# Reordering the first head pair's value products in a two-layer attention block

## The chip, the cores and the metric

The kernel runs on one core of a Trainium2 chip. The metric is the device time of one execution in microseconds, from the runs of the whole kernel; the kernel before takes 861.62 us as the median of three runs (859.24 to 862.12).

A core has a matrix engine (TensorE, PE in the profile), a vector engine (VectorE, DVE), an engine for activation functions and copies (ScalarE, ACT), a general-purpose engine (GpSimd, POOL) and SyncE (SP), which here only issues DMAs. Each engine works through its own queue in order; engines meet through semaphores. TensorE writes to PSUM, of which the kernel uses eight tiles (banks) of 128 x 512 float32 numbers; its other tiles lie in SBUF.

## The reference

Two layers work on 512 tokens of 1024 features, in float32:

```python
for i in range(DEPTH):                       # DEPTH = 2
    hn = rms_norm(x, norm_gain[i])
    y = mixer_a(hn, ...) if i % 2 == 0 else mixer_b(hn, ...)
    x = x + y

def mixer_a(...):                            # 3 groups, 16 heads of 64
    proj = hn @ w_in                         # q, k, v of every group, and the gate
    for g, (window, dilation) in enumerate(((128, 1), (512, 4), (2048, 16))):
        q, k = rms_norm(q) , rms_norm(k)     # for each head
        logits = q @ k.T * scale + bias      # inside the dilated window
        out, lse = softmax(logits) @ v, log of the denominator
    y = sum over g of softmax_g(lse) * out   # merged by denominators
    return (y * silu(gate)) @ w_out
```

`mixer_b` has the same outline with one group and a two-dimensional neighbourhood on an 8 x 64 grid of tokens. The softmax over the three groups of layer A, weighted by their denominators, is the same as one softmax over all keys of the three groups, and the kernel computes it so.

## The kernel before, in words

*Products.* A float32 product is made of three `float32r` ones: each operand is split into a high part (`wh`, `hn_h`) and a rest (`wl`, `hn_l`), and `mm3` adds high x high, high x rest and rest x high in PSUM. I call these three matmuls a triple. The normalised input lies in SBUF in both parts. Weights come in blocks of 1024 columns (`wraw`, eight slots) over SP's queue, some of them added up on the way by GpSimd's DMAs. They are used in 360 *jobs* of 512 (or 384) columns: ScalarE copies the high part, and VectorE or GpSimd subtracts to make the rest. Who does it is chosen at line 165 by the pair in `pool[0]`, set at line 296 by the job's number. A rest is made four jobs ahead of its product.

*Pairs.* Heads go in eight pairs (`hc` 0 to 7). In layer A the first pair is projected plainly (`project_qk`). The others use a scheme of seven block products over the two halves of tokens and of features, with sums of the input (`mix_h`, `mix_l`) and sums of weight blocks; `product` is one of these, eight triples in four jobs, and `put11`, `put12`, `put21`, `put22` and others add it up. `main_a(hc)` runs, in this order: `product`, the gate of the pair before (`gate_a`), `product`, v of the pair before (`v0_a`), four products with mixed inputs, the last `product` with `put21`. For `hc` 1, v of the pair before stands ahead of that last product instead.

*Two streams.* `main` projects; `side` does the attention. `run` steps through `main` and lets `side` in between. TensorE executes in the order in which the program emits. The order is set by a clock in nanoseconds that only counts matmuls (`matmul`, `transpose`; 640 for a triple of 512 columns): `yield n` in `side` means "not before n later", `yield "wait", key, n` means "not before n after the stamp of that key", and `later_on(n, job)` emits a job when the clock has passed n. After the first projection the other engines keep the program's order too. A guard (a key that `main` yields) makes `run` emit everything of `side` up to that stamp at once, whatever its due time.

*The attention of one pair in layer A.* `q_a` transposes q and k on TensorE into a bank of PSUM, four times four 128 x 128 blocks, and copies or subtracts each bank to SBUF (`k0h`, `k0l`, `q0h`, `q0l`, `q12`). `k_a` does the same for k of groups 1 and 2 (`k12`). `attn_a` makes the scores in two halves of four banks (`log`); VectorE adds the bias and takes the minimum (the sign is turned), ScalarE takes the exponential and normalises (`p`), and VectorE turns p in 32 x 32 blocks into `pt`. Four `move`s of four DMAs each bring a part of `pt` into a second tile (`t0`); the last stamps `"pt"`. `v_a` transposes v of group 0. `weigh` makes the products of p with v in three thirds, with a `yield 2200` after each of the first two: two thirds read `pt` in place, with v of groups 1 and 2 (`rawk` in the trace); the last reads the moved tile with the transposed v. It holds four banks (`o`). `weighed` multiplies the result by the gate, and the product goes to DRAM (`y_d`).

`log`, `tp` and `o` banks come in turn from one pool of four (`ps_side`).

*Norms of queries and keys.* `head_norm` computes the inverse root on VectorE, and `scale` multiplies the four token blocks by it, each with a `later_on` of its own (line 438).

*What sets the order around the change.* The last quarter of `main_a(2)`'s first product has the guard `("w", 0)`, since its result overwrites v of the first pair; the stamp comes after `weigh` of the first pair. The fifth product of `main_a(2)` has the guard `("q", 1)`, and v of the second pair has `("scored", 1)`, the second half of that pair's scores. For the first pair alone, `attn_a` has `q_a(1)` ahead of `weigh`:

```python
        if hc == 0:
            yield from q_a(hc + 1)
            yield 2500
        yield "wait", ("pt", hc), 11500 if hc == 1 else 9000 if hc == NHC - 2 else 7500
```

For the other pairs it stands behind. At the end of layer A the stored outputs come back (`y_back`) and are split into high part and rest (`y_split`) for the output projection `out_product`, which waits for each of them.

Of the kernel before, what the change touches and what calls it, by code (L numbers as in the profile page):

```python
# [26 lines left out]
NHC = 8  # L27
# [19 lines left out]
def tile_hybrid_encoder(  # L47
# [24 lines left out]
    held = [False]  # L72
# [41 lines left out]
    def bank(name):  # L114

        return ps_side.tile([P, 512], F32, tag="side", name=name)
# [21 lines left out]
    def rsqrt(eng, r, ss, n, scale):  # L138
        v = wk.tile([P, 32], F32, tag="nv", name="nv", bufs=1)
        a = wk.tile([P, 32], F32, tag="na", name="na")  # L140
        eng.tensor_scalar(v[:, :n], ss, scale, EPS, op0=ALU.mult, op1=ALU.add)
        eng.tensor_scalar(
            r.bitcast(I32), v[:, :n].bitcast(I32), -0.5, float(0x5F3759DF), op0=ALU.mult, op1=ALU.add
        )
        for _ in range(3):
            eng.tensor_mul(a[:, :n], r, r)
            if eng is vec:
                eng.scalar_tensor_tensor(a[:, :n], a[:, :n], -0.5, v[:, :n], op0=ALU.mult, op1=ALU.mult)
                eng.scalar_tensor_tensor(r, a[:, :n], 1.5, r, op0=ALU.add, op1=ALU.mult)
                continue  # L150
            eng.tensor_mul(a[:, :n], a[:, :n], v[:, :n])
            eng.tensor_scalar(a[:, :n], a[:, :n], -0.5, 1.5, op0=ALU.mult, op1=ALU.add)
            eng.tensor_mul(r, r, a[:, :n])

    turn, pool = [0], [[2, 5]]

    def cast(raw, n):
        h = wp.tile([P, 512], F32R, tag="wh", name="wh", bufs=6)[:, :n]
        act.copy(h, raw)
        return h, raw, n  # L160

    def rest(h, raw, n):
        l = wp.tile([P, 512], F32R, tag="wl", name="wl", bufs=5)[:, :n]
        turn[0] += 1
        a, b = pool[0]
        eng = pol if turn[0] * a % b < a else vec
        eng.tensor_sub(l, raw, h.bitcast(F32))
        return h, l
# [11 lines left out]
    class Plan:  # L180
# [28 lines left out]
        def add(self, at, dst, off):  # L209

            dst.used(at)
            src = lambda: w[:, off : off + dst.cols]
            self.sums.setdefault(at, []).append(
                lambda: pol.dma_start(dst.tile, src(), accum_op=ALU.add)
            )
# [39 lines left out]
    mixed_jobs = len(plan.jobs)  # L255
# [23 lines left out]
    def load(raw):  # L279
        home(raw)  # L280
        if raw.off is None:
            return
        dst, src = raw.tile[:, : raw.cols], w[:, raw.off : raw.off + raw.cols]
        if not begun:
            syn.dma_start(dst[:, :512], src[:, :512])
            begun.append(load_x(1, 2))
            dst, src = dst[:, 512:], src[:, 512:]
        syn.dma_start(dst, src)
        if behind:
            behind.pop()()  # L290

    def splits():
        casts, queue, due = [], [], plan.loads(lead)
        for at, (raw, c, step, n) in enumerate(plan.jobs):
            first = at - start_jobs
            pool[0] = [0, 1] if first < 16 else [2, 3] if first < 40 else [1, 2] if at < mixed_jobs else [2, 5]
            for r in due.get(at, ()):
                load(r)
            for add in plan.sums.get(at, ()):
                add()  # L300
            casts.append((cast(raw.tile[:, c : c + step], step), n))
            if len(casts) > 1:
                done, m = casts.pop(0)
                queue.append((*rest(*done), m))
            if len(queue) > 4:
                yield queue.pop(0)
        done, m = casts.pop(0)
        queue.append((*rest(*done), m))
        yield from queue

    def steps():
        for h, l, n in splits():
            for c in range(0, h.shape[1], n):
                yield h[:, c : c + n], l[:, c : c + n]
# [11 lines left out]
    def transpose(o, i):  # L326
        clock[0] += 109
        nc.tensor.transpose(o, i, ident)  # L328
# [15 lines left out]
    def later_on(delay, job):  # L344

        timers.append((clock[0] + delay, job))
        timers.sort(key=lambda t: t[0])
# [75 lines left out]
    def head_norm(raw, ss, ns, late):  # L423


        rs = wk.tile([P, 32], F32, tag="rs", name="rs")
        rsqrt(vec, rs[:, : 4 * ns], ss[:, : 4 * ns], 4 * ns, 1.0 / DH)

        def scale(i):
            by = rs[:, i * ns : (i + 1) * ns].unsqueeze(2).to_broadcast([P, ns, 64])  # L430
            v = raw[:, i, : ns * 64].rearrange("p (a b) -> p a b", b=64)
            return vec.tensor_mul(v, v, by)

        if late:
            later.append(lambda: [tc.keep_in_program_order(scale(i)) for i in range(4)])
            return
        for i in range(4):
            later_on(600 + 600 * i, partial(scale, i)) if held[0] else scale(i)

    def transpose4(raw, c):  # L440
        tp = bank("tp")
        for i in range(4):
            transpose(tp[:, i * P : (i + 1) * P], raw[:, i, c : c + P])
        return tp
# [303 lines left out]
            yield from gate_a(hc)  # L748

    def k_a(hc):  # L750
        yield "wait", ("rawk", hc), 9000 if 1 < hc < NHC - 1 else 12000 if hc < 2 else 8000
        k12 = wk.tile([P, 2, 512], F32, tag="k12", name="k12", bufs=1)
        raw = st.pop(("rawk", hc))
        for g in range(2):
            tp = transpose4(raw, g * P)
            act.activation(k12[:, g, :], tp, AF.Copy, scale=gk[:, g + 1 : g + 2])
            yield
        st["k12", hc] = k12, raw[:, :, 256:]

    def q_a(hc):  # L760

        yield "wait", ("rawq", hc), (22000, 10500)[hc] if hc < 2 else 8000
        raw = st.pop(("rawq", hc))
        q0h = wk.tile([P, 512], F32R, tag="q0h", name="q0h", bufs=1)
        q0l = wk.tile([P, 512], F32R, tag="q0l", name="q0l", bufs=1)
        k0h = wk.tile([P, EXT], F32R, tag="k0h", name="k0h", bufs=1)
        k0l = wk.tile([P, EXT], F32R, tag="k0l", name="k0l", bufs=1)
        q12 = wk.tile([P, 2, 512], F32, tag="q12", name="q12", bufs=1)
        tp = bank("tp")
        for i in range(4):  # L770
            transpose(tp[:, i * P : i * P + P].rearrange("p (r j) -> p j r", j=4), raw[:, i, 3 * P :])
        act.activation(k0h[:, 64:EXT], tp, AF.Copy, scale=gk[:, 0:1])
        yield 1000
        vec.scalar_tensor_tensor(
            k0l[:, 64:EXT], tp, gk[:, 0:1], k0h[:, 64:EXT].bitcast(F32), op0=ALU.mult, op1=ALU.subtract
        )
        yield 400
        tp = transpose4(raw, 0)
        act.copy(q0h, tp)
        yield 1000  # L780
        vec.tensor_sub(q0l, tp, q0h.bitcast(F32))
        yield 400
        for g in range(2):
            act.copy(q12[:, g, :], transpose4(raw, P + P * g))
            yield
        stamp["q", hc] = 0
        st["q", hc] = q0h, q0l, q12, k0h, k0l
# [150 lines left out]
    def attn_a(hc):  # L938
# [7 lines left out]
        at = lambda t, hd: 32 * (4 * hd + t)  # L946
# [115 lines left out]
        if last:  # L1062
# [18 lines left out]
            gt = weighed(hc, (yield from weigh()))  # L1081
# [19 lines left out]
        for u in range(2):  # L1101
            for n, tile_ in enumerate(scores(u)):
                later_on(400 + 900 * n, partial(least, n, tile_))
            if u:
                stamp["scored", hc] = 0
                for n in range(4):
                    later_on(8000 + 2000 * n, partial(move, n))
            yield 8500
        fill = bias_rows() if hc == 2 else None
        yield from v_a(hc)  # L1110
        yield "wait", ("pt", hc), 2500
        st["e", hc + 1] = bias_a(hc + 1)
        if hc == 0:
            yield from q_a(hc + 1)
            yield 2500
        yield "wait", ("pt", hc), 11500 if hc == 1 else 9000 if hc == NHC - 2 else 7500
        yield "wait", ("gate", hc), 4000
        gt = weighed(hc, (yield from weigh()))
        if hc < NHC - 2:
            send = lambda: tc.keep_in_program_order(syn.dma_start(y_d[:, hc, :], gt))  # L1120
            later_on(3000, send)
            stamp["w", hc] = 0
            yield
            if fill:
                later_on(1500, fill)
            if hc:
                yield 1500
                yield from q_a(hc + 1)
            return
        st["tail"], back = y_back(range(2), "tr")  # L1130
        stamp["back",] = 0
# [3 lines left out]
        yield from q_a(hc + 1)  # L1135
        _, more = y_back(range(2, NHC - 2), "rawq")
        for n in range(2, NHC - 2):
            later_on(1000 + 2500 * n, partial(y_split, more[:, n - 2, :], n))
        later_on(16000, partial(y_split, gt, hc))

    pending = []

# [378 lines left out]
```

## Time and profile before

| what | value |
|---|---|
| median of the runs | 861.62 us (859.24 to 862.12) |
| the profiled execution's own time | 864.23 us |
| its span, first to last instruction | 862.5 us |
| mean granted TensorE clock | 0.993 |
| TensorE busy | 833.5 us, 97% |
| VectorE busy | 634.5 us, 74% |
| ScalarE busy | 508.2 us, 59% |
| GpSimd busy | 295.6 us, 34% |
| DMA queue q1 (hardware_dynamic) | 108.78 MB, 40.5% of 16 engines |

How to read the rows shown below. A row of a timeline has the start and the duration in us, the engine, the line, the operation, and output<-inputs by the program's names; in brackets stand the idle time ahead of it and what ended it. Nearly all rows have line 85, 324 or 328, those of the helpers that record them, so the names tell the place. A row of windows has the stretch, its length, the busy time of PE, PEld (weight loads), DVE, ACT and POOL with the number of instructions, the granted TensorE clock, the share of the DMA engines, and GB/s. Ends of matmuls are modelled and overlap the next start, so starts are compared.

### The profile page before, as it was taken

How to read it: one execution, taken by the hardware profiler on the slowest of the kernel's cores; microseconds unless marked ns; L12 is line 12 of the kernel's file. 1: busy time of each engine (PE TensorE's matmuls, PEld its weight loads, DVE VectorE, ACT ScalarE, POOL GpSimd, SP SyncE). 2: the span in 40 equal slices, each digit the busy share in tenths (PEclk: the TensorE clock that was granted, in tenths of full speed). 3: DMA queues.
4: the chain of work that ended last, by engine and by line, in shares of the span. 5: the costliest groups of instructions: out<-in, count | busy, mean ns of one | idle time of the engine just before them, and what ended most of it. 6: DMA issues, size and time to landing. Idle time of an engine off the chain costs nothing.

```text
span 862.5 us, 18120 instructions
## 1 busy us (share of the span) xinstructions
PE 833.5 (97%) x6611; PEld 689.0 (80%) x6611; DVE 634.5 (74%) x1650; ACT 508.2 (59%) x1066; POOL 295.6 (34%) x262
## 2 busy tenths in 40 slices
PE   8998988999999999999999999899999999999998
PEld 6875867878877877878877877689998898889776
DVE  7898994787897787787786866547577667866742
ACT  7565672665764955946846828545366644665440
POOL 5043641363362452443543512212223223322301
PEclk9999998999999999999999999999999999999999
DMA  9425754667766775775776664184264456545212
GB/s 337 135 59 139 203 130 121 126 165 198 146 163 199 149 171 168 159 176 175 163 157 190 137 193 144 56 278 144 86 177 144 119 169 182 160 132 137 83 50 98
DMA packets 56169, 131.97 MB, mean 153 GB/s; under 512 B 7184, under 2 KB 24528, under 8 KB 55952
## 3 DMA queue, kind: packets, MB, share of 16 engines
q1 hardware_dynamic: 49744, 108.78, 40.5%
q0 software_dynamic: 6048, 22.02, 15.2%
q8 instruction: 52, 0.85, 0.4%
q14 instruction: 37, 0.30, 0.1%
q10 hardware_dynamic: 288, 0.01, 0.0%
HBM read 111.73 MB, written 11.72 MB: 143 GB/s over the span
## 4 chain that ended last, share of the span: by engine, by line
PE 69%; DVE 10%; ACT 9%; DMA 5%; issue 5%; POOL 1%; ACTq 0%; DVEq 0%; POOLq 0%; SPq 0%
PE acc L324 57%; ACT p L85 5%; PE o L324 5%; PE log L324 4%; DMA wraw<-in_w 4%; PE tp L328 2%; DVE na L85 2%; DVE wl L85 2%; ACT wh L85 2%; ACT rawk L85 1%; DMA yr<-y_d 1%; DVE p L85 1%; DVE rawq L85 1%; DVE rawk L85 1%; DVE gt L85 1%
## 5 line engine op out<-in xcount | busy, mean ns | idle before, releaser
L85 POOL TENSOR_TENSOR wl<-wraw,wh 128x512 fp32r<-128x512 f32 (+1 forms) x157 | 202.3, 1297 | 432.7 <-PE acc L324 216.7
L85 ACT CAST wh<-wraw 128x512 fp32r<-128x512 f32 (+1 forms) x360 | 209.8, 593 | 195.5 <-PE acc L324 150.3
L85 DVE TENSOR_TENSOR wl<-wraw,wh 128x512 fp32r<-128x512 f32 (+1 forms) x203 | 160.1, 792 | 48.4 <-PE acc L324 32.6
L324 PE MATMUL acc<-wh,hn_h 128*128 128x384 f32 (+1 forms) x488 | 185.9, 381 | 3.6 <-DVE gt L85 1.7
L324 PE MATMUL acc<-wl,hn_h 128*128 128x384 f32 (+1 forms) x488 | 177.5, 364 | 2.3 <-DVE wl L85 2.3
L324 PE MATMUL acc<-wh,hn_l 128*128 128x384 f32 (+1 forms) x488 | 177.3, 363 | 0.0
L85 ACT ACTIVATE p<-p,mn 128x256 f32<-128x256 f32 (+2 forms) x248 | 137.9, 584 | 33.5 <-DVE mn L85 33.5
L324 PEld LDWEIGHTS acc<-wh,hn_h 128*128 128x128 f32 x488 | 92.0, 189 | 21.9 <-issue 6.6
L324 PEld LDWEIGHTS acc<-wl,hn_h 128*128 128x128 f32 x488 | 92.2, 189 | 10.8 <-DVE wl L85 3.4
L324 PEld LDWEIGHTS acc<-wh,hn_l 128*128 128x128 f32 x488 | 92.0, 189 | 9.7
L324 PE MATMUL acc<-wl,mix_h 128*128 128x512 f32 x224 | 87.6, 391 | 2.9 <-DVE wl L85 2.2
L324 PE MATMUL acc<-wh,mix_h 128*128 128x512 f32 x224 | 89.0, 397 | 0.0
L324 PE MATMUL acc<-wh,mix_l 128*128 128x512 f32 x224 | 87.4, 390 | 0.0
L324 PE MATMUL acc<-hn_h,wh 128*128 128x512 f32 x192 | 78.6, 410 | 0.3 <-ACT rawb L85 0.2
L324 PE MATMUL acc<-hn_h,wl 128*128 128x512 f32 x192 | 75.1, 391 | 0.0
L324 PE MATMUL acc<-hn_l,wh 128*128 128x512 f32 x192 | 74.9, 390 | 0.0
L85 DVE STREAM_TRANSPOSE pt<-p 128x512 f32<-128x512 f32 (+1 forms) x60 | 40.4, 686 | 22.9 <-ACT p L85 22.8
L85 DVE TENSOR_REDUCE ss<-sq 128x4 f32<-128x256 f32 (+1 forms) x96 | 46.3, 502 | 12.5 <-POOL sq L85 6.2
L324 PEld LDWEIGHTS acc<-wl,mix_h 128*128 128x128 f32 x224 | 42.1, 188 | 12.8 <-DVE wl L85 3.5
L324 PE MATMUL acc<-y_l,wh 128*128 128x512 f32 x128 | 50.1, 392 | 1.9 <-POOL y_l L85 1.9
L324 PE MATMUL acc<-y_h,wh 128*128 128x512 f32 x128 | 51.8, 405 | 0.0
L324 PE MATMUL acc<-y_h,wl 128*128 128x512 f32 x128 | 50.0, 391 | 0.0
(149 smaller groups left out, 1367.2 us busy)
## 6 DMA issues: line engine op xcount, KB each, us to landing
wraw<-in_w SPq DMA_DIRECT2D x95, 512.0 KB
wraw<-in_w POOLq DMA_DIRECT2D x42, 512.0 KB, 7.0
wraw<-in_w SPq DMA_DIRECT2D x38, 384.0 KB
pt<-pt SPq DMA_DIRECT2D x112, 64.0 KB
td<-tr SPq DMA_DIRECT2D x24, 224.0 KB
pt<-td SPq DMA_DIRECT2D x24, 224.0 KB
e<-l_d SPq DMA_DIRECT2D x32, 112.0 KB
e<-l_d SPq DMA_DIRECT2D x16, 128.0 KB
```

The lines of the kernel that those rows point to most:

```text
L85: m = f(*args, **kw)
L324: nc.tensor.matmul(o, l, r, **kw)
L328: nc.tensor.transpose(o, i, ident)
```

## The change

Four groups of numbers and one step's place are changed.

1. Jobs 16 to 39 after the first sixteen of the kernel: GpSimd makes every second rest instead of two of three.
2. `scale(i)` comes due 600 + 1000 i after the norm instead of 600 + 600 i, where it is timed at all (layer A).
3. First pair: `weigh` comes ahead of `q_a(1)`, which now follows it as for the other pairs, after `yield` and `yield 1500`. The moves come due 1300 apart instead of 2000, and `weigh` 4500 after the stamp `"pt"` instead of 7500.
4. Last pair: `k_a` comes due 9000 after its stamp instead of 8000. The splits of the outputs of pairs 2 to 5 come due 2000 sooner, and so does that of pair 6.

```diff
-            pool[0] = [0, 1] if first < 16 else [2, 3] if first < 40 else [1, 2] if at < mixed_jobs else [2, 5]
+            pool[0] = [0, 1] if first < 16 else [1, 2] if at < mixed_jobs else [2, 5]
...
-            later_on(600 + 600 * i, partial(scale, i)) if held[0] else scale(i)
+            later_on(600 + 1000 * i, partial(scale, i)) if held[0] else scale(i)
...
-        yield "wait", ("rawk", hc), 9000 if 1 < hc < NHC - 1 else 12000 if hc < 2 else 8000
+        yield "wait", ("rawk", hc), 9000 if hc > 1 else 12000
...
-                    later_on(8000 + 2000 * n, partial(move, n))
+                    later_on(8000 + (2000 if hc else 1300) * n, partial(move, n))
...
         st["e", hc + 1] = bias_a(hc + 1)
-        if hc == 0:
-            yield from q_a(hc + 1)
-            yield 2500
-        yield "wait", ("pt", hc), 11500 if hc == 1 else 9000 if hc == NHC - 2 else 7500
+        yield "wait", ("pt", hc), (4500, 11500)[hc] if hc < 2 else 9000 if hc == NHC - 2 else 7500
         yield "wait", ("gate", hc), 4000
...
-            if hc:
-                yield 1500
-                yield from q_a(hc + 1)
+            yield 1500
+            yield from q_a(hc + 1)
             return
...
-            later_on(1000 + 2500 * n, partial(y_split, more[:, n - 2, :], n))
-        later_on(16000, partial(y_split, gt, hc))
+            later_on(2500 * n - 1000, partial(y_split, more[:, n - 2, :], n))
+        later_on(14000, partial(y_split, gt, hc))
```

## The prediction

> **What bounds the kernel now.** I read the page first, then the windows, TensorE's waits, and the timelines of the engines where TensorE loses time.
>
> ```profile
> span 862.5 us, 18120 instructions
> PE 833.5 (97%) x6611; PEld 689.0 (80%) x6611; DVE 634.5 (74%) x1650; ACT 508.2 (59%) x1066; POOL 295.6 (34%) x262
> 188.30:251.40 63.10, 62.91 (x653) 50.60 (x652) 53.07 (x130) 40.11 (x79) 28.48 (x24) 1.00 0.70 168
> 125.00:130.00 5.00, 2.43 (x22) 1.62 (x19) 4.76 (x9) 2.17 (x5) 3.25 (x3) 1.00 0.92 186
> 130.00:135.00 5.00, 2.92 (x90) 2.52 (x98) 3.05 (x7) 0.00 (x0) 0.00 (x0) 0.57 0.45 103
> 135.00:140.00 5.00, 5.00 (x113) 4.42 (x102) 0.88 (x4) 0.09 (x1) 0.00 (x0) 0.75 0.43 141
> 112.00:133.00 21.00, 14.80 (x87) 11.30 (x93) 19.82 (x42) 10.92 (x21) 9.88 (x9) 0.95 0.55 117
> 133.00:150.00 17.00, 17.00 (x233) 14.69 (x226) 4.91 (x11) 5.56 (x10) 2.65 (x2) 0.87 0.45 137
> ```
>
> TensorE (PE) is the bound: 862.5 - 833.5 = 29 us idle in all. One whole head pair in the steady part (188 to 251 us) idles 0.2 us, so nothing in an order of work can earn much there. The idle time lies at the first pair: from 125 to 135 us PE works 5.35 of 10 us, and the granted clock falls to 0.57, then 0.75.
>
> ```profile
> 112.78 0.39 PE L324 MATMUL acc<-wh,hn_h 128*128 128x512 f32 x1
> 118.69 0.39 PE L324 MATMUL acc<-wh,hn_h 128*128 128x512 f32 x1
> 120.62 0.50 PE L324 MATMUL acc<-wl,hn_h 128*128 128x512 f32 x1 [1.55 <-DVE wl L85]
> 125.08 1.47 PE L328 MATMUL tp<-ident,rawq 128*128 128x128 f32 x12
> 126.85 0.93 PE L324 MATMUL o<-pt,rawk 32*64 32x128 f32 x8 [0.29 <-ACT q L85]
> 131.84 0.69 PE L324 MATMUL o<-pt,rawk 32*64 32x128 f32 x4 [4.07 <-DVE k0l L85]
> 132.77 3.67 PE L324 MATMUL o<-pt,rawk 32*64 32x128 f32 x116 [0.24 <-DVE q0l L85]
> 136.37 2.60 PE L324 MATMUL o<-pt,v 128*64 128x64 f32 x64
> 138.90 0.50 PE L324 MATMUL acc<-wh,hn_h 128*128 128x512 f32 x1
> 191.42 1.21 PE L324 MATMUL o<-pt,rawk 32*64 32x128 f32 x64
> 198.22 1.97 PE L324 MATMUL o<-pt,v 128*64 128x64 f32 x60
> ```
>
> The first pair's products with v need the four side banks of PSUM, which the second pair's transposes have just filled; the waits named k0l, q0l and q are those banks being emptied. By the code's clock all of it falls due too late: the guard ("w", 0) ahead of the last quarter of the next product flushes twelve transposes and all the products with v in one lump, with no projection between them.
>
> ```profile
> 115.80 1.18 DVE L85 TENSOR_TENSOR na<-rs 128x32 f32<-128x32 f32 x1
> 117.47 2.50 DVE L85 TENSOR_TENSOR rawq<-rawq,rs 128x512 f32<-128x512 f32 x4
> 119.88 1.28 DVE L85 TENSOR_TENSOR wl<-wraw,wh 128x512 fp32r<-128x512 f32 x2
> 123.93 4.37 DVE L85 SCALAR_TENSOR_TENSOR na<-na,nv 128x16 f32<-128x16 f32 x1
> 131.04 0.74 DVE L85 SCALAR_TENSOR_TENSOR k0l<-tp,gk,k0h 128x512 fp32r<-128x512 f32 x1
> 115.59 1.34 POOL L85 TENSOR_TENSOR wl<-wraw,wh 128x512 fp32r<-128x512 f32 x1 [1.90 <-DVE na L85]
> 124.22 4.03 POOL L85 TENSOR_TENSOR wl<-wraw,wh 128x512 fp32r<-128x512 f32 x3
> ```
>
> Why k0l is late: one 16-column step of the norm takes 4.37 us on DVE, just while POOL runs three subtractions (124.22 to 128.25). GPSIMD Engine Reference, Key points, in the Trainium skill says that POOL shares its SBUF interfaces with VectorE and contends with instructions that have two SBUF inputs; this row agrees: 4.37 us for 16 columns, where a rest of 512 columns takes 0.64.
>
> **The change, part by part.** I count code clock (ns) from the end of the first pair's second scores, at 99.71 us. A triple of matmuls adds 640 and takes 0.68 us: 118.69 - 112.78 = 5.91 us for eight triples and four transposes. v's projection ends at 12160, its transposes stand at 14720.
>
> *Products with v ahead of q_a(1).* The four moves are due at 8000, 9300, 10600 and 11900, so "pt" is stamped at 12160 instead of 14080. Adding 4500 gives 16660, and the products start at 17076, one triple before line 740's product ends. Their second third follows 2200 later, at 20063; the last third is flushed by the guard at 22410. So triples lie between the parts, and no transposes of q_a hold the banks. The three waits go: 4.07 + 0.29 + 0.24 = 4.6 us. The products lasted 138.90 - 131.84 = 7.06 us from the wait's end; a later pair's take 1.21 + 1.21 + 1.97 = 4.4, of which I count 4.3 as elapsed, since groups overlap what follows. That is 2.8 us less, since PE no longer runs at the low clock. Together -7.4 us. q_a(1) now falls due after ("w", 0) + 2700, at 26463, between the gate's triples. Its sixteen transposes cost the same; two more interruptions of triples cost about 0.1 us each, and two more for the thirds of the products: +0.4.
>
> *What is late next* is the last third, which reads the moved tile.
>
> ```profile
> 111.17 1.30 DVE L85 STREAM_TRANSPOSE pt<-p 128x512 f32<-128x512 f32 x2
> 112.49 12.23 SPq L85 DMA_DIRECT2D pt<-pt  x16
> 124.77 6.90 SPq L85 DMA_DIRECT2D e<-l_d  x6
> 112.50:113.50 1.00, 1.00 (x6) 0.81 (x6) 0.81 (x2) 1.00 (x3) 1.00 (x1) 1.00 0.09 16
> 113.50:114.50 1.00, 1.00 (x6) 0.84 (x5) 0.90 (x4) 1.00 (x2) 0.19 (x1) 1.00 0.28 66
> 1.18 4.28 DMA hg<-in_head_gain
> ```
>
> The sixteen moves start when the last stream transpose ends (112.47) and leave SP's queue one after another, 0.76 us each, until 124.72. The closer pacing therefore brings no move forward; it brings the stamp forward. No weight load stands between them now, so none is overtaken; the six bias loads follow as before, and the one weight load behind those, issued at job 34, is first used at job 45. The store to y_d moves forward with the products, ahead of the same loads as now. The last third could start at 112.78 + 14 x 0.68 + 0.36 + 2 x 1.14 = 124.9 us. The first move's bytes show about 1.5 us after its issue (16 GB/s, then 66), so the last lands near 126.2: a new wait of 1.3 us. Ends: 0, if it lands as its issue ends, and 124.72 + 4.28 - 124.9 = 4.1, with the slow constant load as the row. I take 1.3, from the row of the same transfer. DMA: Bandwidth & Descriptors, Anatomy of one DMA, in the Trainium skill gives about 2.0 us fixed cost for a DMA; by that the wait would be 1.8, and the sum 0.5 us smaller.
>
> *Scalings 1000 apart instead of 600.* Only VectorE's order changes. The weight rest that PE awaits at 118.69 stands behind four scalings (2.50 us); it will stand behind two, 1.25 us earlier, and a third of the products (1.14) covers PE meanwhile. The 1.55 us wait goes; ends -0.1 and -1.55, since the next item can put VectorE 1.4 us (two rests) late. In later pairs the last scaling comes 1.2 us later, but its readers wait 8 to 12 us after the stamp: 0, from -1.2 (0.2 us of idle in each of six pairs) to as much lost.
>
> *POOL's share in jobs 16 to 39* falls from 16 rests to 12. Four at about 0.65 us move to VectorE, +2.6 us there at most; four POOL runs of 1.3 us fewer can lock it, 5.2 at most. Rests are made four jobs (5.4 us) ahead, which hides it: 0, from -1 to +2.6.
>
> *The second pair's scores.* k_a(1) follows q_a(1) and moves behind three more triples, while the second scores stay at the guard behind v. Seven triples (4.8 us) instead of ten lie between the two.
>
> ```profile
> 151.86 1.18 PE L324 MATMUL log<-k,q 64*32 64x128 f32 x64
> 160.02 0.38 PE L324 MATMUL log<-k0h,q0h 64*128 64x256 f32 x2
> 157.97 0.48 DVE L85 CUSTOM_DVE_ANT_1 p<-log,e,mn 128x256 f32<-128x256 f32 x1
> ```
>
> VectorE releases the last bank at 158.45, 5.5 us after the first scores end (about 152.97). That leaves a wait of 0.7; ends 0 and 2.2.
>
> *Tail.* Splits of the stored outputs start 2000 clock sooner.
>
> ```profile
> 523.96 0.66 PE L328 MATMUL tp<-ident,rawk 128*128 128x128 f32 x4 [1.66 <-DVE k0l L85]
> 541.50 0.50 PE L324 MATMUL acc<-y_l,wh 128*128 128x512 f32 x1 [0.82 <-POOL y_l L85]
> 549.10 0.50 PE L324 MATMUL acc<-y_l,wh 128*128 128x512 f32 x1 [1.11 <-POOL y_l L85]
> ```
>
> Both y_l waits are shorter than the two microseconds given: -1.9. Ends 0, if ScalarE's exponentials keep them in their place, and -3, if the softmax behind them gains too. k_a's 9000 instead of 8000 for the last pair costs nothing: q_a, ahead of it, ends 10.7 us of clock after that stamp, so the 1.66 stays.
>
> Sum: -7.4 + 0.4 + 1.3 - 1.55 + 0.7 - 1.9 = -8.45 us. The profiled execution took 864.23 us, 2.6 above the median of 861.62. From the median: 853.2 us.
>
> **The rivals.**
>
> *Moves too late.* The last third waits 4.1 us instead of 1.3, about the idle time that lowers the clock now, and the 2.8 us of slow products come back: -8.45 + 2.8 + 2.8 = -2.85, 858.8 us. For it: the DMA engines are 0.92 busy from 125 to 130 us. Against: the moves' own lag of 1.5. TensorE: Matmul & The Clock Gate, Part 1, in the Trainium skill says that the clock halves after an idle window of about 3.4 us; the trace agrees as far as it goes (4.07 lowered it to 0.57, 1.55 did not).
>
> *The gain is given back.* The idle stretch lets VectorE catch up: it is busy 19.82 of 21 us up to 133 and only 4.91 of the 17 after. If rests and norms now run late under a busy PE, PE waits for them one by one; at 8 us of such waits the time is about 861. Against: 24.7 us of VectorE work fit in 38 - 8.5 = 29.5, and the rests that PE needs first stand ahead of the norm.
>
> *VectorE becomes the bound (slower).* A rest moved to VectorE can meet a POOL run and be held:
>
> ```profile
> 85.71 2.88 DVE L85 TENSOR_TENSOR wl<-wraw,wh 128x512 fp32r<-128x512 f32 x1 [1.18 <-ACT wh L85]
> L85 DVE TENSOR_TENSOR wl<-wraw,wh 128x512 fp32r<-128x512 f32 (+1 forms) x203 | 160.1, 792 | 48.4 <-PE acc L324 32.6
> ```
>
> If all four take 2.88 us and nothing hides them, they cost 11.5: -8.45 + 11.5 = +3.05, 864.7 us. It decides from 8.5 us of waits on rests. Against: 203 rests on VectorE take 0.79 us in the mean, so held ones are few, and POOL runs less. The contention rule named above speaks for this rival, for the moved rests have two SBUF inputs.
>
> **How the numbers follow.** 0.3% (2.6 us) is about what a measurement of this kernel can tell from no change. The forecast has 0.62 (849 to 857), moves too late 0.15, a still larger gain in the tail and rests (to 847) 0.05; these are faster, 0.82. Given back: 0.10, same. VectorE bound: 0.08, slower. The range takes in the late moves and part of the given-back case: 848.5 to 860.
>
> **What would show it.** Right: products with v in three groups with triples between, ahead of the second pair's rawq transposes; no wait on k0l near 130 us; granted clock 1.00 throughout 120 to 140; a short wait in the group that reads v; no y_l waits near 540. Wrong: that group waits over 3 us at a lower clock; or new waits on wl from 85 to 145 us; or the second scores wait over 2 us for VectorE.

## The result, and the profile after

The changed kernel takes 857.57 us (median of 8 runs, 854.28 to 860.78), the kernel before takes 862.42 in the runs beside it. The ratio is 0.9942, with a 95% interval of 0.9919 to 0.9965: 4.9 us faster (3.0 to 7.0 by the interval), where 8.45 were forecast. The time lies in the forecast range and the sign is right, but the gain is little more than half of the sum. The profiled execution took 857.42 us, against 864.23 before.

The page of the changed kernel, its first lines:

```profile
span 855.6 us, 18127 instructions
PE 833.8 (97%) x6611; PEld 689.7 (81%) x6611; DVE 636.0 (74%) x1654; ACT 508.8 (59%) x1066; POOL 294.5 (34%) x258
```

TensorE (PE) is as busy as before (833.8 against 833.5 us); the span is shorter because PE idles 21.8 us instead of 29.0. The waits of PE from 100 to 187 us (us in total, number, longest), first in the changed kernel, then in the kernel before (one of 0.2 us that both have is left out):

```profile
PE o L324 <- DMA e<-l_d: 2.9, 1, 2.9
PE o L324 <- DMA pt<-pt: 0.5, 1, 0.5
PE tp L328 <- ACT vt L85: 0.2, 1, 0.2
```

```profile
PE o L324 <- DVE k0l L85: 4.1, 1, 4.1
PE acc L324 <- DVE wl L85: 1.5, 1, 1.5
PE acc L324 <- POOL wl L85: 0.8, 1, 0.8
PE o L324 <- ACT q L85: 0.3, 1, 0.3
PE o L324 <- DVE q0l L85: 0.2, 1, 0.2
```

The waits for banks (k0l, q, q0l) are gone, and so is the wait for a weight rest. One wait is new: the products with v wait for a DMA. The timeline of PE in the changed kernel shows which products (start, length, and in brackets the idle time ahead and who ended it):

```profile
117.56 1.21 PE L324 MATMUL o<-pt,rawk 32*64 32x128 f32 x64
121.71 1.21 PE L324 MATMUL o<-pt,rawk 32*64 32x128 f32 x64
124.79 0.39 PE L324 MATMUL acc<-wh,hn_l 128*128 128x512 f32 x1
128.08 0.58 PE L324 MATMUL o<-pt,v 128*64 128x64 f32 x8 [2.90 <-DMA e<-l_d]
129.15 3.25 PE L324 MATMUL o<-pt,v 128*64 128x64 f32 x56 [0.49 <-DMA pt<-pt]
132.33 0.62 PE L324 MATMUL acc<-wh,hn_h 128*128 128x512 f32 x1
155.41 0.38 PE L324 MATMUL log<-k0h,q0h 64*128 64x256 f32 x2
185.75 1.21 PE L324 MATMUL o<-pt,rawk 32*64 32x128 f32 x64
```

The first two thirds run between triples, without a wait. The last third, which reads the moved tile, is ready when the last triple ends (124.79 + 0.39 = 125.18) and gets going at 128.08 and 129.15. The profile puts the first of these waits down to the bias loads, which go through the same queue right behind the moves. The queue of SyncE (SP), and the vector operation (VectorE, DVE) that the first move waits for:

```profile
113.01 11.47 SPq L85 DMA_DIRECT2D pt<-pt  x16
124.53 6.13 SPq L85 DMA_DIRECT2D e<-l_d  x6
112.28 0.70 DVE L85 STREAM_TRANSPOSE pt<-p 128x512 f32<-128x512 f32 x1
```

The sixteen moves are issued from 113.01 to 124.48, and the products go on at 129.15, 4.7 us after the last issue. Windows of the changed kernel (busy time of each engine, then PEclk, the granted clock of TensorE), and of the two long stretches from the first pair's last projection to the second pair's products with v, in the kernel after and then before:

```profile
125.00:130.00 5.00, 1.61 (x25) 1.31 (x26) 4.59 (x15) 1.34 (x3) 2.13 (x2) 0.92 0.88 198
130.00:135.00 5.00, 5.00 (x57) 4.46 (x54) 2.76 (x9) 1.45 (x3) 0.00 (x0) 0.74 0.48 101
515.00:520.00 5.00, 3.11 (x14) 2.20 (x13) 3.79 (x8) 4.93 (x11) 1.31 (x1) 0.83 0.92 348
520.00:525.00 5.00, 5.00 (x88) 4.00 (x87) 2.15 (x7) 3.81 (x5) 2.38 (x2) 0.83 0.18 67
545.00:550.00 5.00, 3.50 (x109) 2.72 (x116) 3.02 (x9) 1.30 (x3) 0.00 (x0) 0.90 0.39 118
550.00:555.00 5.00, 4.96 (x111) 4.12 (x97) 0.92 (x5) 0.49 (x2) 0.00 (x0) 0.75 0.11 18
111.77:185.75 73.98, 70.15 (x617) 56.27 (x615) 58.47 (x141) 46.28 (x90) 32.10 (x26) 0.98 0.63 147
```

```profile
112.78:191.42 78.64, 71.49 (x618) 57.47 (x616) 57.70 (x137) 45.80 (x88) 32.93 (x27) 0.96 0.55 133
```

The stretch became 4.66 us shorter (78.64 to 73.98). PE's idle time in it fell from 7.15 to 3.83 us (-3.3) and its busy time by 1.3, since less of it runs at a low clock. From 186 us to the last pair's step `k_a` at 517 the two kernels need the same time within 1.1 us (331.5 and 332.5). From there the earlier splits of the stored outputs should have shortened the tail:

```profile
517.22 0.66 PE L328 MATMUL tp<-ident,rawk 128*128 128x128 f32 x4 [1.89 <-DVE k0l L85]
546.28 0.66 PE L328 MATMUL tp<-ident,yr 128*128 128x128 f32 x4 [0.89 <-DVE pt L85]
547.95 3.44 PE L324 MATMUL o<-pt,rawk 32*64 32x128 f32 x126 [0.17 <-DVE pt L85]
551.32 2.58 PE L324 MATMUL o<-pt,v 128*64 128x64 f32 x64
```

In the kernel before, the last two groups of these products stood so:

```profile
558.18 0.47 PE L324 MATMUL o<-pt,rawk 32*64 32x128 f32 x13 [1.26 <-issue]
558.58 2.08 PE L324 MATMUL o<-pt,v 128*64 128x64 f32 x64
```

Both waits for y_l (1.9 us) are gone. But from 517.22 to the end of the last products (553.90) it takes 36.7 us, and before it took 36.7 us too (523.96 to 560.66). A wait for pt grew by 0.7 us. And twice the granted clock fell, from 515 to 525 and from 545 to 555 us, where it was 1.00 before: the way from `k_a`'s step to the first transposes of p became 1.2 us longer apart from the y_l wait, and the products that read v 0.5 us longer. The products with rawk lasted about as long as before (3.4 us after 3.7), since the lower clock replaced a gap of 1.26 us for which the profile names no releaser ("issue").

### The profile page after: what moved, and what is told of

It reads as the page before. It is cut to its first block, busy times and chain, and to the rows that moved or that the text cites. A ratio compares the mean times of both kernels' runs of the same rounds, so it can differ in the third digit from the quotient of the medians.

```text
span 855.6 us, 18127 instructions
## 1 busy us (share of the span) xinstructions
PE 833.8 (97%) x6611; PEld 689.7 (81%) x6611; DVE 636.0 (74%) x1654; ACT 508.8 (59%) x1066; POOL 294.5 (34%) x258
## 4 chain that ended last, share of the span: by engine, by line
PE 74%; DVE 9%; ACT 8%; DMA 4%; issue 3%; SPq 1%; POOL 1%; DVEq 0%; ACTq 0%
PE acc L324 61%; ACT p L85 5%; PE o L324 4%; PE log L324 4%; PE tp L328 3%; DMA wraw<-in_w 2%; DVE wl L85 2%; SPq L85 1%; ACT rawk L85 1%; ACT wh L85 1%; DVE na L85 1%; DVE rawq L85 1%; DVE p L85 1%; DVE gt L85 1%; DMA pt<-in_xt 1%
## 5 line engine op out<-in xcount | busy, mean ns | idle before, releaser
L85 POOL TENSOR_TENSOR wl<-wraw,wh 128x512 fp32r<-128x512 f32 (+1 forms) x153 | 197.6, 1292 | 426.8 <-PE acc L324 227.8
```

What stands on the lines that cost most here:

```text
L85: m = f(*args, **kw)
```

## The experiments

*Theories.* The first: the moved tile is late, and the wait for it with the lowered clock behind it takes most of what is missing. Rivals: the gain is given back elsewhere, by work that now waits under a busy PE; and other parts of the change take back what the reorder brings. Ratios are to the kernel before, with a 95% interval.

**Each part alone.** The reorder alone, on the kernel before (the pace of the moves and the last hunk of `attn_a` belong to it):

```diff
-                    later_on(8000 + 2000 * n, partial(move, n))
+                    later_on(8000 + (2000 if hc else 1300) * n, partial(move, n))
...
-        if hc == 0:
-            yield from q_a(hc + 1)
-            yield 2500
-        yield "wait", ("pt", hc), 11500 if hc == 1 else 9000 if hc == NHC - 2 else 7500
+        yield "wait", ("pt", hc), (4500, 11500)[hc] if hc < 2 else 9000 if hc == NHC - 2 else 7500
```

> The kernel before with the third group of the change alone: the first pair's products with v ahead of the second pair's transposes, moves 1300 apart, 4500 after the stamp. If the gain comes from this step, the time falls by 3 to 5 us against before (the changed kernel: 5 us), the k0l wait of 4.07 us is gone, and the last third waits about 3.4 us for its moves at a lower clock. If the gain comes from the other parts, the time stays within 1 us of before.

The scalings alone, the output splits with the later `k_a` alone, and GpSimd's share alone:

```diff
-            later_on(600 + 600 * i, partial(scale, i)) if held[0] else scale(i)
+            later_on(600 + 1000 * i, partial(scale, i)) if held[0] else scale(i)
```

> The kernel before with the second group alone: scalings 1000 apart. By the prediction the wait of 1.55 us on wl at 118.7 us shrinks to about 0.3 and nothing else moves: 1 to 1.5 us faster. If the spread also frees weight rests in every pair, the steady part's waits go too and the time falls by 2 to 3 us. If the transposes' lump at 125 us absorbs what is gained ahead of it, the time stays within 0.8 us.

```diff
-        yield "wait", ("rawk", hc), 9000 if 1 < hc < NHC - 1 else 12000 if hc < 2 else 8000
+        yield "wait", ("rawk", hc), 9000 if hc > 1 else 12000
...
-            later_on(1000 + 2500 * n, partial(y_split, more[:, n - 2, :], n))
-        later_on(16000, partial(y_split, gt, hc))
+            later_on(2500 * n - 1000, partial(y_split, more[:, n - 2, :], n))
+        later_on(14000, partial(y_split, gt, hc))
```

> The kernel before with the fourth group alone: the last pair's k_a at 9000, output splits 2000 sooner. By the prediction the two y_l waits (0.82 and 1.11 us) go and the time falls by 1.9 us. By the rival, that the wait is given back at the products with v that end layer A (a slower clock or later turns there), the y_l waits go and the time stays within 0.8 us of before.

```diff
-            pool[0] = [0, 1] if first < 16 else [2, 3] if first < 40 else [1, 2] if at < mixed_jobs else [2, 5]
+            pool[0] = [0, 1] if first < 16 else [1, 2] if at < mixed_jobs else [2, 5]
```

> The kernel before with the first group alone: four of GpSimd's rests in jobs 16 to 39 go to VectorE. By the prediction 0 (within 1 us). If fewer GpSimd runs free VectorE from being held, the stretch from 85 to 112 us shortens by about 1 us, as in the changed kernel, and the long VectorE rows (2.88 and 1.70 us) get fewer. If VectorE is the bound there, it is 1 to 2.6 us slower.

| kernel | median us | ratio |
|---|---|---|
| reorder alone | 857.04 | 0.9938 [0.9917, 0.9959] |
| scalings alone | 861.47 | 0.9985 [0.9973, 0.9996] |
| output splits and `k_a` alone | 862.61 | 1.0000 [0.9985, 1.0016] |
| GpSimd's share alone | 862.78 | 1.0005 [0.9988, 1.0022] |
| whole change | 857.57 | 0.9942 [0.9919, 0.9965] |

The reorder alone is as fast as the whole change. GpSimd's share does nothing. The scalings bring 1.3 us (0.3 to 2.3 by the interval), and without the reorder not by the route that I forecast. In the waits from 60 to 140 us of the kernel with the scalings alone the wait for the rest at 118.7 us has shrunk from 1.55 to 0.3 us (the 2.1 us in the list lies ahead of 85 us), but the bank wait named q has grown from 0.3 to 1.6 us:

```profile
PE o L324 <- DVE k0l L85: 4.2, 1, 4.2
PE acc L324 <- DVE wl L85: 2.5, 2, 2.1
PE o L324 <- ACT q L85: 1.6, 1, 1.6
```

What this trace does gain ahead of the second pair lies elsewhere: from the transposes of rawq at 67.5 us to the first pair's second scores it takes 0.6 us less (67.53 to 97.19, before 67.50 to 97.74), where two waits for k of 0.3 and 0.7 us are gone.

The splits alone do in their trace what they are for, and their time still doesn't move. Their timeline, from `k_a`'s step to the last products:

```profile
522.99 0.66 PE L328 MATMUL tp<-ident,rawk 128*128 128x128 f32 x4 [1.39 <-DVE k0l L85]
550.98 0.66 PE L328 MATMUL tp<-ident,yr 128*128 128x128 f32 x4 [0.89 <-DVE pt L85]
555.69 0.47 PE L324 MATMUL o<-pt,rawk 32*64 32x128 f32 x14 [0.95 <-issue]
556.09 2.08 PE L324 MATMUL o<-pt,v 128*64 128x64 f32 x64
```

No wait for y_l is left, one for pt has grown from 0.17 to 0.89 us, and at full clock the stretch takes 35.2 us (522.99 to 558.17) instead of 36.7. Of the 1.5 us that this execution shows, 0.3 is a shorter gap without a releaser between the last products (0.95 instead of 1.26 us); the rest, 1.93 - 0.72 = 1.2 us, is less than the interval of the ratio can tell from nothing (1.3 us on either side).

**The price of the late tile.** The last third of the first pair reads the turned tile in place of the moved one, so nothing in this pair waits for the moves:

```diff
-                        lambda hd, d=run * a + 256 * ia + 32 * ta, m=m: sb(t0, d + 128 * hd, [[m, 2], [1, 32]]),
+                        lambda hd, d=run * a + 256 * ia + 32 * ta, m=m: sb(t0 if hc else pq, d + 128 * hd, [[m, 2], [1, 32]]),
```

> The changed kernel, with the last third of the first pair's products reading the turned tile in place (pq) instead of the moved tile (t0). The moves are still issued, nobody in the first pair waits for them; left out is that these products read the exchanged data. Theory, the wait and the clock cost the rest of the gain: the 2.90 + 0.49 us of waiting in front of the last third go, and so does the low granted clock of 125 to 135 us (o<-pt,v took 4.25 us from start to the next matmul, against 2.0 at full clock), together 5.4 us: about 852 us, ratio to the kernel before near 0.988, granted clock 1.00 from 120 to 135 us, and the second pair's second scores begin near 150 us instead of 155.4. Rival, given back: the work behind the wait (the second pair's scores, which need VectorE) waits in the wait's place, the time stays within 856 to 858 us.

It took 850.66 us, ratio 0.9850 [0.9824, 0.9876]. Its timeline:

```profile
118.12 1.21 PE L324 MATMUL o<-pt,rawk 32*64 32x128 f32 x64
125.69 2.08 PE L324 MATMUL o<-pt,v 128*64 128x64 f32 x64
150.79 0.38 PE L324 MATMUL log<-k0h,q0h 64*128 64x256 f32 x2
181.16 1.21 PE L324 MATMUL o<-pt,rawk 32*64 32x128 f32 x64
```

From the first third to the second pair's products it takes 63.0 us (118.12 to 181.16), in the changed kernel 68.2 (117.56 to 185.75): the late tile costs 5.2 us, of which 3.4 are the wait. The second pair's second scores come 4.6 us earlier and wait for nothing, so this time isn't given back. The clock stayed at 1.00 from 115 to 140 us. The medians differ by more, 6.9 us; in this pair of profiles 1.1 us of the rest lies in the tail, where the clock did not fall behind `k_a`'s step. The first theory stands, and its rival falls.

**What makes it late.** First without the two loads that GpSimd's queue adds up on the way while the moves travel:

```diff
     def add(self, at, dst, off, left_out=False):
             dst.used(at)
+            if left_out:
+                return
...
-                self.add(j + 3 + 2 * i, b11[i], b12[i].off)
+                self.add(j + 3 + 2 * i, b11[i], b12[i].off, hc == 2)
```

> The changed kernel without the two accumulating loads that GpSimd's queue issues at 120.2 and 123.5 us, while the moves travel (left out: the bias slab's two sums of this stage are not added in). Theory, the accumulating loads hold the moves up: the last moved piece lands near 127 instead of 129.15 us, the wait of the last third falls from 3.4 to 1.3 us and the clock is kept, about 853 us. Rival, the issue on SP's queue sets the landing (16 issues, 113.01 to 124.48, 0.72 us each, and some us behind the last): the wait stays at 3.0 to 3.4 us, about 857.5 us.

It took 850.86 us, ratio 0.9863 [0.9838, 0.9888]. Its timeline of SP and of PE:

```profile
113.71 10.64 SPq L85 DMA_DIRECT2D pt<-pt  x16
126.88 2.09 PE L326 MATMUL o<-pt,v 128*64 128x64 f32 x64
```

The moves are issued by 124.35, and at 126.88 the last third needs no wait: the tile is there 2.5 us after the last issue or sooner, against 4.7 in the changed kernel. In the five other profiles of this order that show the landing it came 3.0 to 5.8 us after the last issue, so the accumulating loads are probably a part of the lateness; it is one profile, and whether their 512 KB each or the adding does it isn't separated. (The two sums left out are of weight blocks of the third pair, not of a bias.) A reservation: in this run a rest came 0.86 us late, which put the reader itself back by as much and can hide a wait of that size.

Then with the second pair's bias loads later in the written order:

```diff
-        st["e", hc + 1] = bias_a(hc + 1)
+        if hc:
+            st["e", hc + 1] = bias_a(hc + 1)
...
             stamp["w", hc] = 0
+            if hc == 0:
+                st["e", hc + 1] = bias_a(hc + 1)
```

> The changed kernel with the second pair's six bias loads (e<-l_d, 124.53 to 130.66 us on SP's queue, right behind the moves) issued after the last third instead of ahead of it. Theory, these loads share the DMA engines with the last moves and hold them up: the wait of the last third falls from 3.4 us to 1.5 or less, 854 us or less. Rival, the moves are late by their own issue: the wait stays near 3.4 us and the time near 857.5 us.

```profile
112.76 11.16 SPq L85 DMA_DIRECT2D pt<-pt  x16
124.04 0.50 SPq L85 DMA_DIRECT2D wraw<-in_w  x1
124.59 8.19 SPq L85 DMA_DIRECT2D e<-l_d  x6
126.93 3.34 PE L324 MATMUL o<-pt,v 128*64 128x64 f32 x64 [2.00 <-DMA e<-l_d]
```

855.45 us, ratio 0.9912 [0.9884, 0.9939], between the two expectations. The edit didn't do what it was meant to: SP's queue doesn't wait for the products, so the bias loads left at 124.59 as before, with one weight load put ahead of them. The wait was 2.0 us instead of 3.4 all the same. Whether that is the order of the loads or the scatter of the landing can't be told from this run, so the theory of the bias loads stays untested.

**The last third later.** Instead of making the tile come earlier, this puts more triples ahead of its reader. The stamp `("w", 0)`, at which the guard stops emitting, moves ahead of the last third, so the guard no longer brings it in at once:

```diff
-            yield from side_by_side(mms, 4)
+            if hc:
+                yield from side_by_side(mms, 4)
+                return os
+            for part in range(3):
+                for i in range(16 * part, 16 * part + 16):
+                    ...
+                if part == 1:
+                    stamp["w", hc] = 0
+                if part < 2:
+                    yield (2200, 5000)[part]
             return os
...
-            yield
+            if hc == 0:
+                yield 1000
+            else:
+                yield
             if fill:
                 later_on(1500, fill)
-            yield 1500
+            if hc:
+                yield 1500
             yield from q_a(hc + 1)
```

> The changed kernel with the last third of the first pair's products put 5000 units of the written order behind the second third instead of 2200, the second pair's queries behind it by 1000 instead of 1500. Some 3 us of the gate's triples of 128x512 matmuls thus run ahead of the last third rather than behind it, which begins near 128 us. Theory, the moved tile is late by its landing at 129.15 us: the wait falls from 3.4 to about 1 us and the granted clock stays at 1.00 from 125 to 135 us, 853 to 854 us. Rival, the filling matmuls are missing later: the second pair's second scores wait for VectorE by the same amount, 856 to 858 us.

It took 852.62 us, ratio 0.9877 [0.9854, 0.9901]. Its windows and its timeline:

```profile
125.00:130.00 5.00, 4.80 (x61) 3.84 (x61) 4.59 (x15) 2.48 (x5) 1.82 (x2) 1.00 0.79 166
130.00:135.00 5.00, 5.00 (x49) 4.20 (x44) 3.71 (x10) 1.31 (x2) 1.29 (x1) 1.00 0.51 139
```

```profile
128.21 0.45 PE L324 MATMUL o<-pt,v 128*64 128x64 f32 x8
128.86 1.85 PE L324 MATMUL o<-pt,v 128*64 128x64 f32 x56 [0.20 <-DMA pt<-pt]
```

The wait is 0.2 us and the clock stays at 1.00. The same moves, issued within 0.4 us of the same times and landing as late as before (4.6 us after the last issue), now cost almost nothing. The same kernel once more, as the neighbour of the next three:

> The kernel with the last third put later once more, as the neighbour of the three runs beside it: 852 to 853.5 us, ratio near 0.988.

852.56 us, ratio 0.9884 [0.9866, 0.9902].

**What the other parts are worth with it.** The reorder with the last third later, and nothing else of the change:

> The reorder of the first pair's products alone, with its last third put later; the rawq and rawk scalings, the output splits and the share of GpSimd stay as in the kernel before. Theory, the reorder carries everything once its last third no longer waits: 853 to 854 us, the scalings' 1.3 us being what it lacks. Rival, the other parts pay only where PE is not held by the moved tile: 855 to 857 us, a difference of 3 us or more to the kernel with all parts.

853.70 us, ratio 0.9895 [0.9878, 0.9913]: 1.1 us behind the neighbour, with intervals that overlap, so the reorder carries nearly all of it. Then all parts but the earlier splits:

```diff
-            later_on(2500 * n - 1000, partial(y_split, more[:, n - 2, :], n))
-        later_on(14000, partial(y_split, gt, hc))
+            later_on(1000 + 2500 * n, partial(y_split, more[:, n - 2, :], n))
+        later_on(16000, partial(y_split, gt, hc))
```

> All of the change with the last third put later, but the output splits at the old times. Theory, the earlier splits remove 1.9 us of waits for y_l and bring 0.7 us of waits for pt and, in some runs, a lowered clock of 1.5 to 2 us between 540 and 550 us: without them the time is within 1 us of the neighbour with them, and the granted clock there stays 1.00. Rival, the earlier splits are worth their 1.9 us and tail_alone only failed to show it: the time is 1.5 to 2 us longer than the neighbour's.

853.03 us, ratio 0.9894 [0.9875, 0.9912], 0.5 us from the neighbour. In the neighbour's trace the splits save the waits for y_l and lose the time to the clock:

```profile
541.30 0.66 PE L328 MATMUL tp<-ident,yr 128*128 128x128 f32 x4 [0.89 <-DVE pt L85]
542.97 3.94 PE L324 MATMUL o<-pt,rawk 32*64 32x128 f32 x126 [0.17 <-DVE pt L85]
```

These 126 products take 3.94 us where the kernel with the old splits takes 2.29. Of the eight profiles with the earlier splits (the changed kernel's, and those of seven experiments), four show this lowered clock; of the six with the old splits, none. But a clock of 1.00 doesn't mean 2.29 us: in the other four, and in three of the six with the old splits (the kernel before among them), a gap of 0.6 to 1.3 us without a releaser splits these products, and it takes 3.1 to 3.7 us until the products with v begin. Only three profiles, all with the old splits, show neither. What makes the gap stays open.

At last the same, with one triple moved ahead of the last pair's transposes of rawk:

```diff
-        yield "wait", ("rawk", hc), 9000 if hc > 1 else 12000
+        yield "wait", ("rawk", hc), 9000 if 1 < hc < NHC - 1 else 12000 if hc < 2 else 11000
```

> The kernel with the last third put later, and the last pair's step k_a 2000 units later, so that one triple of the output product runs ahead of its transposes of rawk. Theory, the wait for k0l near 515 us falls from 1.75 to 1.1 us, and the triple is missing behind the last scores, where the transposes of p near 534 us wait 0.7 us longer: no change to the neighbour within 0.7 us. Rival, the shorter wait also keeps the granted clock at 1.00 from 515 to 525 us and the time falls by 1 to 2 us.

850.38 us, ratio 0.9872 [0.9850, 0.9893]. The wait for k0l at 515 us, 1.4 and 1.75 us in the two profiles of the neighbour, is gone altogether, and none has come in its place. From the last transposes of rawq to the end of the last products it takes 35.9 us (510.94 to 546.88), in the neighbour 39.0 (509.91 to 548.92): no change within 0.7 us was expected, and this pair of profiles shows 3.1, of which the wait for k0l is 1.4, two shorter waits for VectorE 0.6, and the products with rawk 0.7. The median is 2.2 us below the neighbour's, but the intervals overlap, and the neighbour's clock stood at 1.00 there anyway: that the rival's mechanism was at work isn't shown. Here the tile landed later again (last third at 129.09, a further wait of 1.07 us):

```profile
113.61 11.19 SPq L85 DMA_DIRECT2D pt<-pt  x16
130.61 1.85 PE L324 MATMUL o<-pt,v 128*64 128x64 f32 x56 [1.07 <-DMA pt<-pt]
```

The kernel with the last third later and the one with the later `k_a` as well are faster than the kernel before and than the changed kernel: their intervals end at 0.990, the changed kernel's begins at 0.992.

## Why the prediction was right, and where it was off

*The reorder, -7.4.* Right in its mechanism: the products run in three groups, the three waits for banks (4.6 us) are gone. Of the 2.8 us for the slow clock, less 0.4 for interruptions, only 1.3 came, since the clock fell again behind the new wait: the last third took 4.25 us (128.08 to 132.33), 0.49 of them waiting.

*The new wait, +1.3.* This is the step that failed, by its size. The time at which PE is ready came out (124.9 forecast, 125.18 measured), by luck: the stretch began 1.0 us earlier than in the kernel before (111.77) and took 13.4 us instead of 12.1. The end of the moves' issue was right (124.72 and 124.48). The lag from issue to landing was not: I took 1.5 us from the time at which the first move's bytes show, when that move had the DMA engines almost to itself, and the tile landed 4.7 us after the last issue. The wait was 3.39 us. The price of about 2.0 us that I quoted stands, under Anatomy of one DMA in DMA: Bandwidth & Descriptors in the Trainium skill, for DMAs issued by GpSimd, while these moves go through SyncE's queue; it would have been too small as well. So the mechanism of the rival *moves too late* (4.1 us of waiting and 2.8 of slow clock) was at work, at a part of its price: the measured gain of 4.85 us lies nearer to that rival's 2.85 than to the forecast 8.45. Why the last moves take so long stays open, but for the probable part of the accumulating loads. The row that spoke for the rival, DMA engines 0.92 busy from 125 to 130 us, doesn't give the lag by itself: with a share of 0.22 there (no accumulating loads) the tile came after 2.5 us or less, with 0.88 (the changed kernel) after 4.7, but with 1.00 (bias loads later) after 3.0.

*The rest's wait, -1.55.* Gone, as forecast (in the kernel with the reorder alone it shrinks to 0.2 us as well, so the reorder by itself takes most of it). *Second scores, +0.7.* They waited for nothing. A wait of 0.8 us for a rest from GpSimd, which I had not counted, went too. So the stretch came to -4.66 where these steps summed to -7.4 + 0.4 + 1.3 - 1.55 + 0.7 = -6.55: +2.1 for the wait, about +1.1 for the clock, -0.7 and -0.8, and 0.2 for a new short wait for vt.

*The tail, -1.9.* Wrong in what it is worth. The y_l waits went as forecast, 0.7 us came back as a wait for pt, and in this execution the lowered clock took the rest (1.2 us of it between 517 and 538 us). Alone and in the faster kernel the step is worth nothing that can be measured.

*GpSimd's share and `k_a`, 0.* Right for GpSimd's share; at `k_a` the 1.66 us at k0l stayed (1.89), but this time the clock fell behind it.

*The rivals.* *Given back* is refuted for the reorder: with the late tile priced out, its gain stays. *VectorE becomes the bound* didn't happen: TensorE waits for no rest from 85 to 187 us. Measured against the median, -4.66 and 0 for the tail make -4.7, and the medians differ by 4.85. The profiled executions differ by 6.8; the further 2 us lie before 112 us and in the steady part, where two profiles of one and the same program (the kernel with the last third later) differ by 1.8 us between the products of the second and of the seventh pair.

## What to carry to other kernels

When a reorder brings the reader of a DMA forward, don't take the landing from the first transfer of the series, and allow for scatter: the last of sixteen moves landed 2.5 us or less to 5.8 us after its issue. Here it was enough to put independent work ahead of the reader instead of hurrying the transfer: 3 us of triples in front of the last third brought 5 us. And price a step by what its stretch gains, not by the waits that go: the y_l waits went in every kernel with the earlier splits, and the time did not follow measurably.

## What I had not expected of the hardware

The granted clock fell behind waits much shorter than the 4.07 us that lowered it before: in the changed kernel behind one of 1.89 us (0.83 from 515 to 525 us, where PE had worked 3.11 of 5 us), and near 545 us behind a run of short ones, 0.89, 0.44 and 0.17 us (down to 0.75). Over the fourteen profiles, from 40 to 560 us, no wait of up to 1.80 us lowered it, runs of short waits and waits with a longer one close behind apart; all of 2.90 us or more did; and of those from 1.86 to 2.35 us some did and some did not. One and the same wait for a rest near 81 us, 2.12 to 2.14 us long in nine profiles, lowered it in six (0.69 over the 5 us behind) and left it at 1.00 in three. The run of short waits left it at 1.00 in the kernel with the splits alone. TensorE: Matmul & The Clock Gate, Part 1, in the Trainium skill speaks of an idle window of about 3.4 us that runs freely, so that it counts where in it the work falls; the change from run to run agrees with that, the length doesn't, for waits of 1.86 to 2.20 us lowered it too. What decides it these runs don't settle.

The landing of the moved tile scattered more than its issue. In the changed kernel it came 4.7 us after the last issue, in the kernel with the later `k_a` 5.8 (124.80 to 130.61), in the kernel with the bias loads later 3.0, in the kernel without the accumulating loads 2.5 or less.

The prediction reads the 4.37 us step of the norm on VectorE as a step with two inputs that GpSimd's subtractions hold up. In the kernel with the reorder alone an earlier step of the same norm, which has one tensor input (`rs<-nv`, 128 x 16), took 4.54 us at the same place (123.82, beside three subtractions from 124.28 to 128.31) and 0.17 at 65 us. So here it isn't only steps with two tensor inputs that are held.
